# Three buffers for the modulation's weight tiles, and twelve K chunks of layer 0's output projection in three passes, in a two-layer hybrid decoder trunk

## Chip, cores and metric

The kernel runs on one core of a Trainium2 chip, as one program. The metric is the device time of the whole program in microseconds. Beside it stands the profile of one execution, from which all waits and busy times are read.

## What is computed

Two layers over 256 tokens of width 2048, all in float32. Each layer has a token mixer and a SwiGLU FFN, both behind an RMSNorm that is modulated by a conditioning vector. The mixer has three groups side by side (gated linear attention, sliding-window attention, gated DeltaNet), and one output projection.

```python
def reference(x, c, positions, w_mod, b_mod, ...):
    c_act = jax.nn.silu(c)
    for l in range(DEPTH):
        mod = c_act @ w_mod[l] + b_mod[l]
        shift1, scale1, gate1, shift2, scale2, gate2 = jnp.split(mod[:, None, :], 6, axis=-1)
        h = rms_norm(x, norm1_gain[l]) * (1.0 + scale1) + shift1
        x = x + gate1 * hybrid_token_mixer(h, positions, w_in[l], ..., w_out[l])
        h = rms_norm(x, norm2_gain[l]) * (1.0 + scale2) + shift2
        x = x + gate2 * swiglu_ffn(h, ffn_w_gate[l], ffn_w_up[l], ffn_w_down[l])
    return rms_norm(x, final_norm_gain)
```

In the mixer, `proj = h @ w_in` is cut into the groups' inputs, the group outputs are joined to 2048 columns (GLA the first 512, attention the next 1024, DeltaNet the last 512), and `mix @ w_out` follows. The GLA's decay comes from 16 columns of the projection times a 16 x 256 matrix, `gla_w_gk`.

## The kernel before

*Projections.* `stream` (a `gemm` is a stream of one group) walks over the 16 K chunks of 128 rows of a weight matrix. For each it loads 128 rows by 1024 columns (512 KB) into a `raw` tile, and multiplies for both 128-token blocks and both 512-column segments, that is four products, summed over K in PSUM tiles `acc` (L358). There are two ways to do a chunk:

- three passes: ScalarE rounds the tile to fp32r (`wh`, L330), VectorE takes the rest (`wl`, L331), and TensorE adds three products of high and low parts, 12 instructions a chunk;
- whole: the raw tile is used as it is in fp32, one product each, which the chip runs as two instructions. Then the tiles of `wh` and `wl` serve as landing places of raw weights too, in turn with `raw` (three each).

`WHOLE_OUT` says which 512-row groups of the output projection are whole: before, all four of layer 0 (0 GLA, 1 and 2 attention, 3 DeltaNet) and none of layer 1. The projection is done in two streams of two column halves each: K chunks 4 to 15, while the GLA is still running, then 0 to 3. For a group in three passes the activations are split too (`split_mix`, L392 and L393).

*Modulation.* `mod_segment` takes 16 steps for 1024 columns. Each loads a tile of `w_mod` of 512 KB (`mraw`, L220, pool `modp`) and adds it, times a value of c per partition, to `acc` on VectorE (L223, 128x1024). At the end, TensorE sums over partitions (L248, or L238 for gates, whose split also takes an `mraw` tile). The segments wait in a list (`mods`), and `tick` takes one out at a rate per weight chunk, so the modulation of later sub-layers is spread over the projections. Layer 0's first gate and second shift and scale (96 steps) must be done by its second norm.

*What sets the order.* All DMAs stand in one queue, SP's, and are issued strictly in its order: a load whose buffer is not free holds back all that stand behind it. The tile framework's scheduler decides in which order the instructions of each engine stand (the code's order is not it), so a pool's number of buffers moves instructions on every engine. The work that meets in the stretch of this change is the DeltaNet (its last VectorE row is L735), the sliding-window heads (L898 to L920), the last input projection (raw tiles 128x528), the GLA (L761 its product with `wgk`, then L764 to L842, levels L795, L798, L799, L804, L823, L831, and L515 at the end of each block), the output projection with its gated sum (L929, L931), and the second norm (L422, L441 to L451).

*Memory.* `kp` holds tiles for good: constants, `ones`, a rounded copy `ones_r`, the per-layer `small`, and `wgk` (the GLA's 16 x 256 matrix), loaded by `load_small` at the start of a layer.

Of the kernel before, what the change touches and what calls it, by code (L numbers as in the profile page):

```python
# [10 lines left out]
F32 = mybir.dt.float32  # L11
# [4 lines left out]
AF = mybir.ActivationFunctionType  # L16
# [3 lines left out]
P = 128  # L20
D = 2048
T = 256
# [20 lines left out]
WHOLE_IN = (True, False)  # L43
WHOLE_A = (3, 0)
RATE_LAST = 1.6
WHOLE_OUT = ((0, 1, 2, 3), ())
XN_ACT = ((False, False), (False, False))

FIN_LAG = 4
# [54 lines left out]
def trunk(ctx: ExitStack, tc, x, cT, pos, small, consts, b_mod, w_mod, w_in, w_gk, w_out,  # L104
# [2 lines left out]

    kp = ctx.enter_context(tc.tile_pool(name="kp", bufs=1))
    rawp = ctx.enter_context(tc.tile_pool(name="rawp", bufs=3))
    modp = ctx.enter_context(tc.tile_pool(name="modp", bufs=2))  # L110
    wsp = ctx.enter_context(tc.tile_pool(name="wsp", bufs=3))
    accp = ctx.enter_context(tc.tile_pool(name="accp", bufs=2))
    gatep = ctx.enter_context(tc.tile_pool(name="gatep", bufs=2))
# [13 lines left out]
    def tl(pool, shape, tag, dt=F32, bufs=None):  # L127
        return pool.tile(shape, dt, tag=tag, name=nm(tag), bufs=bufs)
# [11 lines left out]
    V, A, G, TE, SY = nc.vector, nc.scalar, nc.gpsimd, nc.tensor, nc.sync  # L140
# [19 lines left out]
        return ct[:, o:o + w] if o < N_FULL else masks[:, o - N_FULL:o - N_FULL + w]  # L160

    ident = cst("ident")
    ones = tl(kp, [P, P], "ones")
    G.memset(ones, 1.0)
    ones_r = tl(kp, [P, P], "ones_r", F32R)
    A.activation(ones_r, ones, AF.Copy)
    eps_t = tl(kp, [P, 1], "eps")
    G.memset(eps_t, EPS)
    half = tl(kp, [P, 16], "half")
# [287 lines left out]

    scr = [None, None]

    small_t, wgk_t = {}, {}  # L460
    gains = tl(kp, [P, DEPTH, 2 * KD], "gains")
    SY.dma_start(gains, small[:, :, :2 * KD].rearrange("l p n -> p l n"))

    def load_small(l):
        small_t[l] = tl(kp, [P, SMALL_W], "small")
        SY.dma_start(small_t[l], small[l][:, 2 * KD:])
        wgk_t[l] = tl(kp, [16, 256], "wgk")
        SY.dma_start(wgk_t[l], w_gk[l])

    def sm(l, name):  # L470
        o, w = SMALL[name]
# [17 lines left out]
    def to_mix(l, key, ps, gain=None):  # L489
        if key[1] == 0 and 0 not in WHOLE_OUT[l]:  # L490
            mix[key] = split(ps, gain)
# [37 lines left out]
    def gdn(l, pool, pc, zg, cbca):  # L529
# [3 lines left out]
        for gi, name in enumerate("qkv"):  # L533
            for c2 in range(2):
                ps = bank()
# [49 lines left out]
        ps = bank()  # L585
        for ni, name in enumerate("qk"):
            for c2 in range(2):
                sq = tl(pool, [P, 2, T], "g")
                A.activation(sq, hat[name, c2], AF.Square)
                for c in range(2):  # L590
                    for blk in range(NB):
                        n = ni * 8 + blk * 4 + c2 * 2 + c
                        TE.matmul(ps[:, n:n + 1], sq[:, c, blk * P:(blk + 1) * P],
                                  ones[:, 0:1], start=True, stop=True)
        ss = tl(smp, [P, 16], "qkss")
        V.tensor_scalar(ss, ps[:, :16], EPS, None, ALU.add)
        norms = tl(smp, [P, 8], "knorm")
# [12 lines left out]
        for blk in range(NB):  # L610
            ps = bank()
# [12 lines left out]
        for blk in range(NB):  # L624
# [4 lines left out]
            ps = bank()  # L629
# [7 lines left out]
            if blk == 0:  # L637
                ps = bank()
# [6 lines left out]
            else:  # L645
                ps = bank()
# [5 lines left out]
            ps = bank()  # L652
            for h in range(4):
                TE.matmul(ps[:, h * P:(h + 1) * P], ch("k", h, blk), ch("k", h, blk),
                          start=True, stop=True)
# [3 lines left out]
            ps = bank()  # L659
            for h in range(4):  # L660
                TE.matmul(ps[:, h * P:(h + 1) * P], ch("k", h, blk), ch("q", h, blk),
                          start=True, stop=True)
# [10 lines left out]
        for m in LEVELS[1:]:  # L673
            for blk in range(NB):
                ps = bank()
# [5 lines left out]
                ps = bank()  # L681
# [13 lines left out]
        for blk in range(NB):  # L695
            rhs = v_tok[blk]
            if blk == 1:
                ps = bank()
# [7 lines left out]
            ps = bank()  # L706
# [5 lines left out]
            if blk == 0:  # L712
                ps = bank()
# [5 lines left out]
                ps = bank()  # L719
# [4 lines left out]
            else:  # L724
                ps = bank()
# [5 lines left out]
                ps = bank()  # L731
# [6 lines left out]

    def gla(l, pool, qk_tok, v_tok, zg, lr):

        chan = []
        for i in range(2):
            ps = bank("ga")
# [10 lines left out]
        ps = bank("ga")  # L754
        for blk in range(NB):
            TE.transpose(ps[:16, blk * P:(blk + 1) * P], lr[blk], ident)
        lrT = tl(pool, [16, T], "lrT", bufs=1)
        A.activation(lrT, ps[:16, :T], AF.Copy)
        ps = bank("ga")
        for blk in range(NB):  # L760
            TE.matmul(ps[:, blk * T:(blk + 1) * T], lrT[:, blk * P:(blk + 1) * P], wgk_t[l],  # L761
                      start=True, stop=True)
        z = tl(pool, [P, NB, T], "a")
        V.tensor_tensor(z, ps.rearrange("p (b c) -> p b c", b=NB), bc(sm(l, "b_gk"), NB, 1),  # L764
# [7 lines left out]
        ps = bank("ga")  # L772
# [62 lines left out]
        for blk in range(NB):  # L835
            ps = bank("ga")
            for h in range(4):
                o = ps[:, h * P:(h + 1) * P]
                if blk == 1:
                    TE.matmul(o, cross[:, h % 2, h // 2], v_tok[0][:, h * P:(h + 1) * P],  # L840
                              start=True, stop=False)
                TE.matmul(o, Am[h % 2][:, h // 2, blk], v_tok[blk][:, h * P:(h + 1) * P],  # L842
                          start=blk == 0, stop=True)
# [374 lines left out]
```

## Time and profile before

| | us |
|---|---|
| median of 3 runs | 2584.6 |
| lowest, highest | 2583.5, 2589.6 |
| the profiled execution | 2585.3 |
| its span in the profile | 2583.5 |

Busy shares of the span: TensorE 94%, its weight loads 73%, VectorE 66%, ScalarE 41%, GpSimd 2%. HBM moved 233 GB/s on average, 600.8 MB in all.

How to read it: names like `acc<-wh,hm` are output and inputs in the program's names, L numbers are lines of the kernel before. In the wait views a line says who waited, for whom, how long in total, how often and the longest. In the stretch view a line gives the stretch, its length, then the busy time of TensorE (PE), its weight loads (PEld), VectorE (DVE), ScalarE (ACT) and GpSimd (POOL) with instruction counts, the granted TensorE clock as a share, the DMA engines' busy share and GB/s. SPq is SP's queue of DMAs.

### The profile page before, as it was taken

Reading aid. Unit: us, or ns where it says so; the run is one execution under the profiler, and the core shown is the slowest. Engines: PE = TensorE matmul, PEld = TensorE weight load, DVE = VectorE, ACT = ScalarE, POOL = GpSimd, SP = SyncE. Lnnn points to the kernel's source line nnn. Section 1 sums busy time; section 2 is a strip of 40 time slices with the busy share of each in tenths; the row PEclk is TensorE's granted clock in tenths of the full one; section 3 lists DMA queues with packets and bytes.
Section 4 is the critical chain, followed back from the end, with each engine's and each line's share of the span. In section 5 each row is a group of like instructions: output and inputs, shape, how many; then the busy total and the mean of one; then the engine's idle time right before and its main releaser. Section 6 shows DMA issues by size and latency. Waiting matters only on the chain.

```text
span 2583.5 us, 30803 instructions
## 1 busy us (share of the span) xinstructions
PE 2432.7 (94%) x11164; PEld 1884.1 (73%) x11164; DVE 1714.4 (66%) x2171; ACT 1053.5 (41%) x1548; POOL 58.2 (2%) x117
## 2 busy tenths in 40 slices
PE   4999998889999988999999999999999999999998
PEld 2555785447878767788877878877778878888876
DVE  6767867576675777657578785888664575544555
ACT  2203443124444333344335454564644434344443
POOL 1000000000000000000000000000000000000000
PEclk9999999989999999999999999999999999999999
DMA  9996538777778888868687861675676686666654
GB/s 341 368 322 204 180 114 282 258 231 268 261 259 260 283 268 274 292 193 286 223 277 261 281 192 50 214 232 192 212 256 193 200 286 195 188 191 188 189 184 155
DMA packets 190033, 600.79 MB, mean 233 GB/s; under 512 B 21628, under 2 KB 26268, under 8 KB 189496
## 3 DMA queue, kind: packets, MB, share of 16 engines
q1 hardware_dynamic: 189880, 598.81, 70.7%
q8 instruction: 88, 1.44, 0.2%
q14 instruction: 65, 0.53, 0.1%
HBM read 596.63 MB, written 2.10 MB: 232 GB/s over the span
## 4 chain that ended last, share of the span: by engine, by line
PE 57%; DMA 20%; DVE 10%; issue 8%; ACT 4%; POOL 1%; SPq 1%; DVEq 0%; ACTq 0%; POOLq 0%
PE acc L358 48%; DMA mraw<-in_w_mod 13%; DVE wl L331 4%; DMA raw<-in_w_down 3%; DMA raw<-in_w_in 2%; DVE acc L223 2%; ACT wh L330 1%; PE mm L403 1%; PE ga L895 1%; DMA raw<-in_w_up 1%; PE mm L678 1%; PE mm L685 1%; PE ga L916 1%; DMA raw<-in_w_gate 1%; PE fin L248 1%
## 5 line engine op out<-in xcount | busy, mean ns | idle before, releaser
L358 PE MATMUL acc<-wh,hm 128*128 128x512 f32 (+3 forms) x4872 | 1339.2, 389 | 20.9 <-DVE xs L931 4.7
L330 ACT ACTIVATE wh<-raw 128x1024 fp32r<-128x1024 f32 (+3 forms) x669 | 684.7, 1025 | 985.8 <-PE acc L358 548.9
L331 DVE TENSOR_TENSOR wl<-raw,wh 128x1024 fp32r<-128x1024 f32 (+3 forms) x669 | 785.2, 1179 | 446.6 <-ACT wh L330 444.5
L358 PEld LDWEIGHTS acc<-wh,hm 128*128 128x128 f32 x4872 | 892.0, 189 | 215.8 <-issue 25.5
L358 PE MATMUL acc<-wl,hm 128*128 128x512 f32 (+3 forms) x2484 | 792.3, 394 | 12.2 <-DVE wl L331 9.7
L223 DVE SCALAR_TENSOR_TENSOR acc<-mraw,c_act,acc 128x1024 f32<-128x1024 f32 x320 | 410.3, 1282 | 225.2 <-DMA mraw<-in_w_mod 222.9
L358 PEld LDWEIGHTS acc<-wl,hm 128*128 128x128 f32 x2484 | 458.4, 190 | 124.1 <-DVE wl L331 22.3
L358 PE MATMUL acc<-wh,ahl 128*128 128x512 f32 x560 | 158.4, 397 | 0.0
L358 PEld LDWEIGHTS acc<-wh,ahl 128*128 128x128 f32 x560 | 105.8, 189 | 24.5
L358 PE MATMUL acc<-wl,ahl 128*128 128x512 f32 x280 | 90.8, 398 | 7.2 <-DVE wl L331 7.2
L223 DVE SCALAR_TENSOR_TENSOR g<-g,c_act,g 128x512 f32<-128x512 f32 x128 | 88.7, 747 | 12.6 <-DMA g<-in_w_mod 12.4
L358 PE MATMUL acc<-wh,b 128*128 128x512 f32 (+2 forms) x184 | 74.7, 545 | 2.2 <-ACT b L447 2.1
L358 PE MATMUL acc<-wl,b 128*128 128x512 f32 (+2 forms) x176 | 67.1, 518 | 2.6 <-DVE g L969 2.6
L358 PEld LDWEIGHTS acc<-wl,ahl 128*128 128x128 f32 x280 | 52.2, 189 | 23.1 <-DVE wl L331 11.3
L358 PE MATMUL acc<-raw,b 128*128 128x512 f32 (+2 forms) x176 | 67.6, 524 | 0.0
L358 PEld LDWEIGHTS acc<-wh,b 128*128 128x128 f32 x184 | 35.2, 197 | 30.8 <-issue 23.1
L358 PEld LDWEIGHTS acc<-wl,b 128*128 128x128 f32 x176 | 32.8, 192 | 29.2 <-issue 20.3
L416 ACT ACTIVATE acc<-xs 128x512 f32<-128x512 f32 x32 | 19.0, 595 | 85.7 <-DVE xs L931 85.7
L447 ACT ACTIVATE b<-mm,mod,mod 128x128 f32<-128x128 f32 x24 | 9.2, 461 | 109.7 <-DVE mod L256 92.1
L358 PEld LDWEIGHTS acc<-raw,b 128*128 128x128 f32 x176 | 33.5, 195 | 26.7 <-issue 21.7
L929 DVE TENSOR_TENSOR acc<-acc,gate 128x512 f32<-128x512 f32 x64 | 43.0, 695 | 10.3 <-PE acc L358 10.2
L358 PE MATMUL acc<-raw,hm 128*128 128x512 f32 x88 | 41.7, 598 | 1.4 <-ACT acc L416 1.4
(314 smaller groups left out, 1645.8 us busy)
## 6 DMA issues: line engine op xcount, KB each, us to landing
mraw<-in_w_mod SPq DMA_DIRECT2D x320, 512.0 KB
raw<-in_w_down SPq DMA_DIRECT2D x176, 512.0 KB
raw<-in_w_gate SPq DMA_DIRECT2D x160, 512.0 KB
raw<-in_w_up SPq DMA_DIRECT2D x160, 512.0 KB
raw<-in_w_in SPq DMA_DIRECT2D x72, 512.0 KB
g<-in_w_mod SPq DMA_DIRECT2D x128, 256.0 KB
raw<-in_w_out SPq DMA_DIRECT2D x43, 512.0 KB
raw<-in_w_in SPq DMA_DIRECT2D x32, 264.0 KB
```

The costliest lines, as they stand in the source:

```text
L223: V.scalar_tensor_tensor(acc, raw[:, a], c_act[:, i + a:i + a + 1], acc, ALU.mult, ALU.add)
L248: TE.transpose(ps[:, i * P:(i + 1) * P], acc[:, (j + i) * P:(j + i + 1) * P], ident)
L330: A.activation(wh[:, :width], raw[:, :width], AF.Copy)
L331: V.tensor_tensor(wl[:, :width], raw[:, :width], wh[:, :width].bitcast(F32), ALU.subtract)
L358: TE.matmul(ps[blk, j][:, :segs[j][2]], xa, parts[j][part], start=i == 0 and n == 0, stop=last and n == len(terms) - 1)
L403: TE.transpose(ps[:, j * P:(j + 1) * P], src[:, j * P:(j + 1) * P], ident)
L416: A.activation(scr[0]() if junk is None else junk, xs[:, blk, j * 512:(j + 1) * 512], AF.Square, accum_out=ssq[blk][:, j:j + 1])
L678: TE.matmul(ps[:, s], LT[blk][:, s], Tm[blk][:, s], start=True, stop=True)
L685: TE.matmul(ps[:, s], U[blk][:, s], m1[:, s], start=True, stop=True)
L895: TE.matmul(ps[:, j * nk:(j + 1) * nk], qT[rows, i + j], kT[rows, g, :nk], start=True, stop=True)
L916: TE.matmul(ps[:, j * 64:(j + 1) * 64], pT[:, j * nk + kb * P:j * nk + (kb + 1) * P], kv[kb][:, P + g * 64:P + (g + 1) * 64], start=kb == ...
L929: V.tensor_tensor(ps, ps, need(gate_row, (l, part, j)), ALU.mult)
```

## The change

`modp` gets a third buffer. `WHOLE_OUT` for layer 0 keeps only group 0 whole, so twelve of sixteen chunks go through three passes. `ones` goes (`ones_r` is set to 1.0 directly and read as fp32 where `ones` was), and `wgk` moves into the GLA's own pool, loaded at the start of `gla`.

```diff
-WHOLE_OUT = ((0, 1, 2, 3), ())
+WHOLE_OUT = ((0,), ())
...
-    modp = ctx.enter_context(tc.tile_pool(name="modp", bufs=2))
+    modp = ctx.enter_context(tc.tile_pool(name="modp", bufs=3))
...
-    ones = tl(kp, [P, P], "ones")
-    G.memset(ones, 1.0)
     ones_r = tl(kp, [P, P], "ones_r", F32R)
-    A.activation(ones_r, ones, AF.Copy)
+    G.memset(ones_r.bitcast(F32), 1.0)
...
     def load_small(l):
         small_t[l] = tl(kp, [P, SMALL_W], "small")
         SY.dma_start(small_t[l], small[l][:, 2 * KD:])
-        wgk_t[l] = tl(kp, [16, 256], "wgk")
-        SY.dma_start(wgk_t[l], w_gk[l])
...
-                                  ones[:, 0:1], start=True, stop=True)
+                                  ones_r[:, 0:1].bitcast(F32), start=True, stop=True)
...
     def gla(l, pool, qk_tok, v_tok, zg, lr):
 
+        wgk = tl(pool, [16, T], "wgk", bufs=1)
+        SY.dma_start(wgk, w_gk[l])
...
-            TE.matmul(ps[:, blk * T:(blk + 1) * T], lrT[:, blk * P:(blk + 1) * P], wgk_t[l],
+            TE.matmul(ps[:, blk * T:(blk + 1) * T], lrT[:, blk * P:(blk + 1) * P], wgk,
```

The scheduler orders all engines anew. Lines after the change are two to four less than before (L220 is L218, L331 is L329, L323 is L321, L804 is L802). Three places show it. The first is SP's queue in layer 0, where the last input projection's loads (`raw` 128x528) meet the modulation's (`mraw`). Before:

```order
L323 DMA raw_2860<-in_w_in 128x528
L323 DMA raw_2881<-in_w_in 128x528
L323 DMA raw_2899<-in_w_in 128x528
L220 DMA mraw_2814<-in_w_mod 128x1024
L220 DMA mraw_2839<-in_w_mod 128x1024
L220 DMA mraw_2878<-in_w_mod 128x1024
L220 DMA mraw_2917<-in_w_mod 128x1024
L220 DMA mraw_2956<-in_w_mod 128x1024
L323 DMA raw_2920<-in_w_in 128x528
```

After, at the same loads (2856, 2877 and 2895 are 2860, 2881 and 2899 of before):

```order
L321 DMA raw_2856<-in_w_in 128x528
L218 DMA mraw_3012<-in_w_mod 128x1024
L218 DMA mraw_3051<-in_w_mod 128x1024
L321 DMA raw_2877<-in_w_in 128x528
L218 DMA mraw_3090<-in_w_mod 128x1024
L738 DMA wgk_3171<-in_w_gk 16x256
L218 DMA mraw_3137<-in_w_mod 128x1024
L218 DMA mraw_3452<-in_w_mod 128x1024
L218 DMA mraw_3455<-in_w_mod 128x1024
L321 DMA raw_2895<-in_w_in 128x528
```

The modulation's loads stood behind these weight loads and now stand between and ahead of them; by the end of the input projection seven more are issued. The GLA's small load stands among them.

The second is VectorE's queue at one level of layer 0's GLA (L804 and L795 are the level's products and differences, L831 its masked copies). Before:

```order
L795 TENSOR_TENSOR a_3260<-a_3186 128x512
L250 TENSOR_REDUCE sums_889_3476<-fin_3477 128x4
L223 SCALAR_TENSOR_TENSOR acc_3433<-mraw_3508,c_act_102,acc_3433 128x1024
L831 COPY_PREDICATED a_3188<-masks_90,ga_3248 128x512
L831 COPY_PREDICATED a_3189<-masks_90,mm_3249 128x512
L804 TENSOR_TENSOR a_3264<-a_3163,a_3260 128x32x8
L804 TENSOR_TENSOR a_3264<-a_3156,a_3260 128x32x8
```

After:

```order
L793 TENSOR_TENSOR a_3263<-a_3208 128x512
L221 SCALAR_TENSOR_TENSOR acc_3479<-mraw_3662,c_act_100,acc_3479 128x1024
L329 TENSOR_TENSOR wl_3671<-raw_3668,wh_3670 128x1024
L829 COPY_PREDICATED a_3210<-masks_90,ga_3251 128x512
L829 COPY_PREDICATED a_3211<-masks_90,mm_3252 128x512
L802 TENSOR_TENSOR a_3267<-a_3185,a_3263 128x64x4
L802 TENSOR_TENSOR a_3267<-a_3178,a_3263 128x64x4
```

A split of the output weights (L329, before L331) now stands beside the modulation's multiply inside the level.

The third is SP's queue in layer 0's FFN, in the third pair of gate and up projections. Before, a run without modulation:

```order
L323 DMA raw_5553<-in_w_gate 128x1024
L323 DMA raw_5571<-in_w_gate 128x1024
L323 DMA raw_5589<-in_w_gate 128x1024
L323 DMA raw_5628<-in_w_gate 128x1024
L323 DMA raw_5646<-in_w_gate 128x1024
L323 DMA raw_5667<-in_w_gate 128x1024
```

After:

```order
L218 DMA mraw_6235<-in_w_mod 128x1024
L321 DMA raw_5785<-in_w_gate 128x1024
L321 DMA raw_5803<-in_w_gate 128x1024
L218 DMA mraw_6274<-in_w_mod 128x1024
L321 DMA raw_5824<-in_w_gate 128x1024
L321 DMA raw_5842<-in_w_gate 128x1024
L218 DMA mraw_6331<-in_w_mod 128x1024
```

Modulation loads now stand here, one in three; eleven more are issued by the first load of the down projection.

More of the change, by code (lines that the diff above doesn't have):

```diff
@@ L458, in trunk @@
     scr = [None, None]
-    small_t, wgk_t = {}, {}
+    small_t = {}
     gains = tl(kp, [P, DEPTH, 2 * KD], "gains")
```

## Prediction

> **What bounds the kernel now.** I read the page first (busy time, the chain), then stretches of busy time for each stage, then the waits in those stretches, and last the order of instructions before and after.
>
> ```profile
> span 2583.5 us, 30803 instructions
> ...
> PE 2432.7 (94%) x11164; PEld 1884.1 (73%) x11164; DVE 1714.4 (66%) x2171; ACT 1053.5 (41%) x1548; POOL 58.2 (2%) x117
> PE 57%; DMA 20%; DVE 10%; issue 8%; ACT 4%; POOL 1%; SPq 1%; DVEq 0%; ACTq 0%; POOLq 0%
> PE acc L358 48%; DMA mraw<-in_w_mod 13%; DVE wl L331 4%; DMA raw<-in_w_down 3%; DMA raw<-in_w_in 2%; DVE acc L223 2%; ACT wh L330 1%; PE mm L403 1%; PE ga L895 1%; DMA raw<-in_w_up 1%; PE mm L678 1%; PE mm L685 1%; PE ga L916 1%; DMA raw<-in_w_gate 1%; PE fin L248 1%
> ```
>
> TensorE is busy for 94% of the span, so the whole kernel has 151 us of TensorE idle time to give (2583.5 less 2432.7). What stands out in the chain is 13% in loads of modulation weights: the stages in which those loads run are the ones to look at. The next view gives busy time by stretch (length, then PE, PEld, DVE, ACT, POOL, granted clock, DMA share, GB/s): first layer 0's mixer from the end of the delta rule to the second norm, then the same stretches of layer 1 (first edge the VectorE row L735, then L764, the second L515 of the GLA, the first L422 of the norm), then the others.
>
> ```profile
> 363.70:413.50 49.80, 45.73 (x311) 38.82 (x310) 36.07 (x55) 26.31 (x61) 2.76 (x4) 1.00 0.78 249
> 413.50:474.10 60.60, 55.00 (x257) 29.41 (x257) 45.82 (x71) 18.90 (x40) 3.98 (x3) 1.00 0.86 293
> 474.10:560.90 86.80, 75.80 (x186) 33.53 (x184) 57.97 (x70) 7.96 (x17) 1.90 (x2) 0.96 0.80 261
> 1618.70:1701.00 82.30, 79.26 (x482) 65.98 (x480) 63.41 (x90) 45.98 (x101) 6.91 (x9) 0.98 0.69 219
> 1701.00:1766.40 65.40, 59.97 (x353) 47.03 (x354) 59.15 (x85) 36.79 (x58) 2.94 (x2) 1.00 0.62 203
> 1766.40:1810.30 43.90, 40.42 (x175) 31.63 (x174) 35.46 (x50) 22.14 (x35) 0.96 (x1) 1.00 0.65 216
> ...
> 160.00:290.00 130.00, 122.96 (x456) 75.62 (x455) 94.71 (x212) 41.64 (x87) 5.19 (x6) 0.93 0.66 219
> 600.00:1110.00 510.00, 484.54 (x2103) 388.49 (x2101) 347.95 (x316) 201.06 (x208) 3.81 (x4) 0.99 0.82 273
> 1110.00:1290.00 180.00, 179.59 (x815) 147.78 (x814) 112.59 (x106) 75.82 (x79) 1.91 (x2) 1.00 0.73 235
> 1400.00:1500.00 100.00, 94.08 (x544) 80.45 (x543) 75.47 (x118) 47.45 (x69) 0.00 (x0) 1.00 0.89 286
> 1676.00:1830.00 154.00, 139.59 (x753) 111.71 (x752) 125.15 (x181) 90.96 (x163) 5.96 (x6) 0.97 0.60 198
> 2060.00:2130.00 70.00, 67.29 (x305) 55.24 (x304) 49.62 (x46) 27.89 (x29) 0.00 (x0) 1.00 0.84 287
> ```
>
> In layer 0's output projection (474 to 561) TensorE works 75.8 of 86.8 us on one-instruction-pair fp32 products, and VectorE is free for a third of the time. Within it, the chain alternates for 35 us between a modulation load and the multiply that frees its buffer:
>
> ```profile
> 481.93 5.50 DMA mraw<-in_w_mod
> ...
> 511.26 4.29 DMA mraw<-in_w_mod
> 515.55 0.03 issue
> 515.60 0.04 issue
> 515.65 1.30 DVE acc L223
> ```
>
> From 481.93 to 511.26 there are five such turns, 5.87 us each, and each moves two modulation tiles and about one of the output weights: two buffers set that pace. In layer 0's FFN (600 to 1110) 25.5 us of TensorE are idle, against 0.4 us in 1110 to 1290. Who waits there:
>
> ```profile
> PEld acc L358 <- DVE wl L331: 22.3, 26, 2.4
> SPq L323 <- DVE wl L331: 320.2, 165, 4.2
> SPq L220 <- DVE acc L223: 31.7, 28, 2.1
> ACT wh L330 <- DMA raw<-in_w_down: 68.9, 30, 5.7
> DVE acc L223 <- DMA mraw<-in_w_mod: 93.8, 68, 3.6
> ```
>
> VectorE stands 93.8 us in a multiply whose tile has not landed; the split for the next weights (L331) is queued behind it, and TensorE waits for the split.
>
> **The change, part by part.** Durations:
>
> ```profile
> 488.72 3.60 PE L358 MATMUL acc<-wl,hm 128*128 128x512 f32 x8
> 492.15 3.60 PE L358 MATMUL acc<-raw,hm 128*128 128x512 f32 x8
> 2236.02 86.31 PE acc L358 x379
> 475.30 0.66 PE ga L403 x4
> L331 DVE TENSOR_TENSOR wl<-raw,wh 128x1024 fp32r<-128x1024 f32 x605 | 736.7, 1223 | 435.6 <-ACT wh L330 434.3
> L223 DVE SCALAR_TENSOR_TENSOR acc<-mraw,c_act,acc 128x1024 f32<-128x1024 f32 x320 | 410.3, 1282 | 225.2 <-DMA mraw<-in_w_mod 222.9 <-DMA acc<-in_b_mod 0.2
> L393 DVE TENSOR_TENSOR hm<-hm,hm x6: 682/684/686, 1673.4 to 1687.4; 128x512 fp32r<-128x512 f32 x6
> ```
>
> *Split on TensorE.* One chunk by one half in whole fp32 is four products, eight instructions, and starts 3.43 us after the one before it (492.15 less 488.72). In three passes it is twelve at 0.228 us (86.31/379), 2.73 us. Twelve chunks by two halves: 24 x 0.70 = 17 us less TensorE work. The Trainium skill ("FP8 and Floating Point Precision", TensorE Precision Notes) says that true FP32 makes four passes through the array; at 0.228 us each that would be 3.65 us a step and 22 us saved. The rows say 3.43, so 17 stands.
>
> *Split on VectorE and ScalarE.* 24 x 1.223 + 6 x 0.684 = 33.5 us more VectorE work, and about as many ScalarE instructions; ScalarE is busy 8 of 87 us there and takes them. VectorE is strict in its order, so I added up the rows of both orders between the same edges: VectorE's each at its mean duration from the groups (means include overlap, so sums run up to a tenth over busy time), TensorE's at 0.228 us for 512 columns in one pass, 0.858 (3.43/4) in whole fp32 and 0.165 (0.66/4) for a 128-column fp32 product. VectorE before: 39.1, 51.0, 61.6 us in the three stretches; after: 50.9, 66.2, 63.9. TensorE before 42.3, 48.8, 77.3; after 50.4, 46.4, 59.9. The largest of the two per stretch comes to 170.6 before and 181.0 after: TensorE's 17 us are outdone by VectorE.
>
> How much longer than that sum the stretches last is the open size. Before it is 197.2/170.6 = 1.16; at the same ratios, stretch by stretch, after would take 59.9 + 78.7 + 71.8 = 210. Layer 1 already splits its whole output projection; its VectorE sums are 68.4, 66.3 and 38.5 for 82.3, 65.4 and 43.9 us. At those ratios after takes 61.2 + 65.3 + 72.9 = 199. With no slack at all it would be 181. I take layer 1's, since it is the same code with the same splits: 199 against 197, +2. Bounds -16 and +13.
>
> *Modulation moved ahead.* Seven modulation steps now stand before L735 and two A-projection splits after it.
>
> ```profile
> 320.00:360.00 40.00, 39.82 (x285) 34.25 (x283) 21.25 (x40) 18.04 (x51) 2.41 (x4) 1.00 0.11 28
> ```
>
> From 320 to 360 DMA runs at 28 GB/s and VectorE is half free, while TensorE is dense: cover for 7 x 1.28 us. TensorE's rows ahead of L734 shrink by 6.6 us (moved behind it). So L735 comes between 6.6 us earlier (TensorE sets it) and 9 us later (every added multiply sits in the delta rule's serial chain); I take 5 earlier, as TensorE is at 99.6%. With the +2 the mixer gives -3, between -23 and +22. From the first L422 on, the second norm's rows are the same: nothing.
>
> *Layer 0's FFN.* Of 25.5 us idle, at most the waits for L331 (22.3 at the weight loads, which overlap other work) can go; the rest are fill and evacuation. With a third buffer a modulation tile is issued one step earlier in SP's order, and the 93.8 us of waiting multiplies, 1.4 us each over 68, mostly land within one more turn. Bounds 0 and -20; I take -8, a third of the idle time, since SP's own waits are ten to one for weight tiles (320.2 against 31.7) and the third buffer does not touch those. Eleven modulation steps also leave the down projection's stretch for the gate and up stretch.
>
> *160 to 290* (last input block, same two-buffer turns): 7.0 us idle, between 0 and -7, I take -2. *Layer 1* (1400 to 1500, 1676 to 1830, 2060 to 2130): 5.9 + 14.4 + 2.7 = 23 us idle, but weights rather than modulation are late in most of it and its VectorE sums hardly change (173.2 before, 173.8 after); between +3 and -10, I take -3.
>
> *The rest.* The dropped copy of the ones (one 128x128 ScalarE instruction) stood under the load of x at the start:
>
> ```profile
> 2.12 8.08 DMA xs<-in_x
> ```
>
> so it is worth nothing. The GLA's small weight load (16 KB, two in all) moves to SP's queue among the A projection's loads. In layer 0 it waits for a ScalarE square of the delta rule's last gate; behind it stand ten weight loads that TensorE needs. At that place SP already waits for buffers and TensorE does not notice (39.82 of 40 above), and the load's user stands just ahead of the edge at 413.5, a whole stretch later: nothing, at worst one SP turn of 5 us. In layer 1 it waits for nothing.
>
> Sum: -2 - 3 - 8 - 3 = -16 against the profiled execution's 2585.3 us (span 2583.5, 1.8 us around it; 0.7 above the median of 2584.6): 2569.
>
> **Rivals.** *VectorE becomes the bound in the GLA (slower).* The GLA is a serial chain VectorE, ScalarE, TensorE, VectorE, level by level; in front of each level there now stand a multiply and a split, 2.5 us, where there was a multiply alone. Before, VectorE is already full in the middle of it:
>
> ```profile
> 440.00:460.00 20.00, 17.92 (x98) 9.39 (x96) 19.44 (x33) 5.75 (x10) 0.95 (x1) 1.00 0.91 316
> ```
>
> If the ratios of before hold (210) and the earlier multiplies delay the delta rule by 9 us, the mixer loses 13 + 9 = 22, and with -13 from elsewhere the kernel takes 2594. It decides from the point where L735 to L422 takes over some 216 us. Against it: layer 1's GLA, as loaded (66.3), takes 65.4. The Trainium skill ("TensorE: Matmul & The Clock Gate", in the section on the array's sub-arrays) calls ScalarE and VectorE strict FIFOs; the multiplies that wait 93.8 us with splits behind them agree, and it is what makes this rival possible.
>
> *The third buffer changes nothing.* SP is held by weight tiles, and a modulation load that stands behind one goes no earlier, whatever its buffer. Then early, FFN and layer 1 terms are zero and only the mixer's -3 stays: 2582. For it: 320.2 against 31.7 us of SP waits. Against it: the turns of 5.87 us, where SP waits for the multiply.
>
> *All slack goes.* The last stretch stops turning on two buffers and lasts its 64 us of VectorE rows, the mixer gives -20, the FFN -14, the early part -4, layer 1 -5: 2542. For it: all three resources (60 us TensorE, 64 VectorE) are even there. Against it: no stretch of either layer's mixer but layer 1's GLA comes within a tenth of its sum.
>
> **How the numbers follow.** My forecast 0.55, VectorE-bound 0.13, no effect of the buffer 0.20, all slack 0.12. About 0.3% (7.75 us) can be told from no change. Faster: 0.9 of the forecast's chance, all of the last, a fifth of the third: 0.65. Slower: the first rival and a little: 0.14. Same: 0.21. The forecast's own range is 2558 to 2580; for 8 in 10 it must reach most of both outer cases: 2546 to 2592.
>
> **What would show it.** Right: in layer 0, L735 to L422 about 199 us, L735 at about 359; the DMA share from 320 to 360 well above 0.11; 24 more 128x1024 rows of L331; fewer whole fp32 products; VectorE's waits for modulation tiles in the FFN at half of 93.8 us or less, TensorE idle there near 17 us. Wrong: the GLA over 72 us long (first rival); FFN waits unchanged (second); the mixer's last stretch under 66 us (third). A changed time in 1110 to 1290, where nothing is moved, would mean a cause that I have not seen.

## The result, and the profile after

The changed kernel takes 2563.9 us (median of 4 runs, 2560.5 to 2566.4), the kernel before 2584.1 beside it (2578.1 to 2589.6): ratio 0.9916, 95% interval 0.9892 to 0.9940, 20 us faster. The forecast was 2569, range 2546 to 2592. Total and sign held; of the terms that made them up, most were mis-sized, and one lay outside its bounds. One run of the kernel with only the room, below, took 7672 us and is left out of its median. The profiled execution after took 2560.5 us, 24.8 less than the one profiled before, so the stages below add up to 24.8 and not to 20.

Head and two groups of the page after (weight splits, modulation's multiplies):

```profile
span 2558.7 us, 31074 instructions
...
PE 2412.8 (94%) x11260; PEld 1903.4 (74%) x11260; DVE 1745.6 (68%) x2201; ACT 1079.6 (42%) x1576; POOL 58.3 (2%) x117
...
L329 DVE TENSOR_TENSOR wl<-raw,wh 128x1024 fp32r<-128x1024 f32 (+3 forms) x693 | 815.4, 1181 | 472.9 <-ACT wh L328 471.0
L221 DVE SCALAR_TENSOR_TENSOR acc<-mraw,c_act,acc 128x1024 f32<-128x1024 f32 x320 | 409.9, 1281 | 133.2 <-DMA mraw<-in_w_mod 130.8
```

VectorE's idle time in front of the modulation's multiplies fell from 225.2 to 133.2 us, and VectorE has 31 us more work (1714.4 before). Busy time by stretch after, with edges at the same instructions as before: the last input block up to the first mask of the delta rule (L680 before, L676 now), the stretch inside the delta rule, the mixer's three stretches (L731 to L762, to the GLA's second L513, to L420), layer 0's FFN, and the stretch in which nothing is moved.

```profile
160.00:276.60 116.60, 113.61 (x430) 67.11 (x429) 90.00 (x207) 39.61 (x84) 4.73 (x6) 0.99 0.69 231
320.00:360.00 40.00, 37.93 (x258) 32.56 (x257) 27.03 (x51) 20.85 (x59) 2.90 (x6) 1.00 0.47 135
349.50:406.40 56.90, 54.47 (x360) 46.74 (x360) 47.11 (x71) 36.08 (x83) 2.20 (x5) 1.00 0.81 256
406.40:475.20 68.80, 56.12 (x319) 44.34 (x319) 58.94 (x88) 32.40 (x53) 4.92 (x4) 0.88 0.64 206
475.20:554.40 79.20, 63.61 (x199) 38.58 (x198) 59.91 (x68) 14.47 (x24) 1.79 (x2) 0.91 0.77 269
593.00:1085.00 492.00, 478.76 (x2109) 390.11 (x2108) 349.41 (x317) 200.93 (x209) 3.83 (x4) 0.99 0.83 283
1085.00:1265.00 180.00, 178.96 (x812) 147.55 (x811) 113.00 (x106) 75.38 (x79) 1.91 (x2) 1.00 0.73 235
```

The waits after in 593 to 1085, which answer to those shown of before in the FFN:

```profile
PEld acc L356 <- DVE wl L329: 6.4, 8, 1.6
SPq L321 <- DVE wl L329: 328.2, 171, 5.7
SPq L218 <- DVE acc L221: 29.3, 25, 1.9
DVE acc L221 <- DMA mraw<-in_w_mod: 66.0, 51, 3.3
```

Stage by stage, in us of the two profiled executions:

| stage | before | after | shift | forecast |
|---|---|---|---|---|
| start to the first L680 | 289.7 | 276.6 | -13.1 | -2 |
| L680 to L735 (delta rule) | 74.0 | 72.9 | -1.1 | -5 |
| L735 to L422 (GLA, output projection) | 197.2 | 204.9 | +7.7 | +2 |
| L422 to the end of layer 0 (FFN) | 805.6 | 787.7 | -17.9 | -8 |
| layer 1 and the end | 1217.0 | 1216.6 | -0.4 | -3 |

### The profile page after: what moved, and what is told of

It is laid out like the page before. It is cut to its first block, busy times and chain, and to the rows that moved or that the text cites. A ratio compares the mean times of both kernels' runs of the same rounds, so it can differ in the third digit from the quotient of the medians.

```text
span 2558.7 us, 31074 instructions
## 1 busy us (share of the span) xinstructions
PE 2412.8 (94%) x11260; PEld 1903.4 (74%) x11260; DVE 1745.6 (68%) x2201; ACT 1079.6 (42%) x1576; POOL 58.3 (2%) x117
## 3 DMA queue, kind: packets, MB, share of 16 engines
q1 hardware_dynamic: 189880, 598.81, 71.1%
## 5 line engine op out<-in xcount | busy, mean ns | idle before, releaser
L356 PE MATMUL acc<-wh,hm 128*128 128x512 f32 (+3 forms) x5000 | 1363.3, 386 | 28.5 <-ACT wh L328 13.8
L329 DVE TENSOR_TENSOR wl<-raw,wh 128x1024 fp32r<-128x1024 f32 (+3 forms) x693 | 815.4, 1181 | 472.9 <-ACT wh L328 471.0
L328 ACT ACTIVATE wh<-raw 128x1024 fp32r<-128x1024 f32 (+3 forms) x693 | 710.4, 1027 | 1007.2 <-PE acc L356 616.8
L356 PEld LDWEIGHTS acc<-wh,hm 128*128 128x128 f32 x5000 | 916.1, 189 | 220.3 <-ACT wh L328 19.0
L356 PE MATMUL acc<-wl,hm 128*128 128x512 f32 (+2 forms) x2516 | 794.8, 389 | 9.4 <-DVE wl L329 7.9
L356 PEld LDWEIGHTS acc<-wl,hm 128*128 128x128 f32 x2516 | 464.8, 189 | 111.5 <-DVE wl L329 17.2
L221 DVE SCALAR_TENSOR_TENSOR acc<-mraw,c_act,acc 128x1024 f32<-128x1024 f32 x320 | 409.9, 1281 | 133.2 <-DMA mraw<-in_w_mod 130.8
L356 PE MATMUL acc<-raw,b 128*128 128x512 f32 (+2 forms) x176 | 66.7, 517 | 0.0
L356 PEld LDWEIGHTS acc<-wl,ahl 128*128 128x128 f32 x280 | 52.5, 189 | 16.3 <-DVE wl L329 4.1
L929 DVE TENSOR_TENSOR xs<-xs,acc 128x512 f32<-128x512 f32 x64 | 41.5, 678 | 0.0
L210 POOL MEMSET acc<- 128x1024 f32 x20 | 19.0, 955 | 961.3 <-PE fin L246 651.2
```

The lines of the kernel that those rows point to most:

```text
L210: G.memset(st["acc"][:, :width], 0.0)
L221: V.scalar_tensor_tensor(acc, raw[:, a], c_act[:, i + a:i + a + 1], acc, ALU.mult, ALU.add)
L328: A.activation(wh[:, :width], raw[:, :width], AF.Copy)
L329: V.tensor_tensor(wl[:, :width], raw[:, :width], wh[:, :width].bitcast(F32), ALU.subtract)
L356: TE.matmul(ps[blk, j][:, :segs[j][2]], xa, parts[j][part], start=i == 0 and n == 0, stop=last and n == len(terms) - 1)
L929: V.tensor_tensor(x_j, x_j, ps, ALU.add)
```

## The experiments

Five questions: which part of the change gains, why the other part costs, whether VectorE's work or the weights' landing places are behind that cost, what the third buffer does in the FFN, and what the one queue of loads costs. All kernels stand beside runs of the kernel before (2581 to 2584 us in each set). Intervals are of the ratio to it.

| kernel | median | ratio, 95% interval |
|---|---|---|
| room only (two buffers, no split) | 2578.8 | 0.9987, 0.9969 to 1.0005 |
| third buffer alone | 2548.6 | 0.9864, 0.9840 to 0.9888 |
| split alone | 2586.8 | 1.0016, 1.0000 to 1.0031 |
| the change (both) | 2563.9 | 0.9916, 0.9892 to 0.9940 |
| split, fourth raw buffer for the third modulation buffer | 2581.2 | 0.9997, 0.9980 to 1.0013 |
| third buffer, landing in raw only | 2549.7 | 0.9865, 0.9838 to 0.9892 |
| the same, with splits that nobody reads | 2563.7 | 0.9925, 0.9900 to 0.9951 |
| third buffer, second half split | 2561.9 | 0.9913, 0.9889 to 0.9936 |
| two buffers, modulation steps moved | 2577.9 | 0.9980, 0.9962 to 0.9998 |
| the change, earlier modulation | 2551.6 | 0.9885, 0.9861 to 0.9908 |
| third buffer alone, earlier modulation | 2555.8 | 0.9898, 0.9874 to 0.9922 |
| third buffer, four chunks split | 2545.7 | 0.9861, 0.9837 to 0.9886 |
| the change, modulation in GpSimd's queue | 2649.2 | 1.0262, 1.0233 to 1.0292 |

How far one profiled execution can be trusted: layer 1 does the same work in all of these but the last, and its part of the span reads 1217 to 1229 us. Some profiled executions lie well off their kernel's median (the split alone 2596.3 against 2586.8, the third buffer alone 2555.2 against 2548.6). A single stage is taken as different below only where several kernels agree or where medians say it.

### The parts alone

Room only:

```diff
-WHOLE_OUT = ((0,), ())
+WHOLE_OUT = ((0, 1, 2, 3), ())
...
-    modp = ctx.enter_context(tc.tile_pool(name="modp", bufs=3))
+    modp = ctx.enter_context(tc.tile_pool(name="modp", bufs=2))
```

> Only the room made for the buffer: the ones tile dropped and the small GLA matrix loaded inside the GLA, two modulation buffers, whole fp32 in all of layer 0's output projection, as before. Theory A (third buffer) and theory B (split) both expect the time of before, 2584 us within 5, and L735 at about 364 us. Theory C (the moved small load and the new order of instructions are what gains): 2572 or less, with L735 near 350.

Third buffer alone, against the changed kernel:

```diff
-WHOLE_OUT = ((0,), ())
+WHOLE_OUT = ((0, 1, 2, 3), ())
```

> Third modulation buffer, no split: all of layer 0's output projection stays whole fp32. Theory A (the third buffer gives the gain, in the early input blocks and in layer 0's first down projection, the split gives next to nothing): 2560 to 2569 us, L735 14 us earlier than before, the first down projection some 17 us shorter, L735 to L422 about 197 us or less as VectorE has fewer splits. Theory B (the 17 us of TensorE work saved by the split are the gain): 2580 us or more, L735 earlier but the time given back at the whole-fp32 output projection.

Split alone:

```diff
-    modp = ctx.enter_context(tc.tile_pool(name="modp", bufs=3))
+    modp = ctx.enter_context(tc.tile_pool(name="modp", bufs=2))
```

> The split alone, two modulation buffers. Theory A: 2580 to 2592 us, L735 at about 364, L735 to L422 197 to 210 us with VectorE the busiest engine, waits of multiplies for modulation tiles in layer 0's FFN at 90 us or more as before. Theory B: 2563 to 2570 us, L735 to L422 about 180 us.

The room cannot be told from no change (2578.8). From there the third buffer gives 30 us by the medians (2548.6; 32 by the ratios). By the medians the split costs 8 us with two buffers (2586.8, intervals just overlapping) and 15 with three (2563.9 against 2548.6; the runs, 2560 to 2566 and 2542 to 2555, do not overlap). So the change is a gain of 30 and a loss of 15. Theory A held for the buffer, though its 2560 to 2569 us was too slow, and it missed the loss. Theories B and C fell. The rows of the mixer (L735 to L422) and of the FFN, first room only, then the third buffer alone:

```profile
360.00:559.80 199.80, 179.74 (x751) 102.88 (x749) 139.72 (x194) 53.09 (x118) 8.64 (x9) 0.97 0.80 264
559.80:1361.10 801.30, 768.08 (x3343) 619.57 (x3344) 542.75 (x519) 329.99 (x378) 9.07 (x11) 0.98 0.78 260
```

```profile
349.60:538.40 188.80, 179.33 (x783) 106.84 (x783) 138.18 (x197) 56.78 (x130) 8.04 (x11) 0.99 0.79 268
538.40:1327.50 789.10, 762.13 (x3344) 615.91 (x3343) 540.54 (x513) 330.58 (x379) 8.13 (x10) 0.99 0.79 265
```

The changed kernel's mixer in one row, and that of the split alone:

```profile
349.50:554.40 204.90, 174.19 (x875) 129.66 (x875) 165.95 (x225) 82.96 (x160) 8.91 (x10) 0.93 0.73 244
```

```profile
359.50:562.50 203.00, 168.09 (x847) 122.04 (x845) 166.67 (x221) 78.72 (x147) 6.49 (x9) 0.95 0.77 254
```

The third buffer brings the mixer from 199.8 to 188.8 without the split, and nothing with it (203.0, 204.9). TensorE's busy time times its granted clock is 179.33 x 0.99 = 177.5 with the buffer alone and 174.19 x 0.93 = 162.0 after: 15.5 us less work by this estimate, near the 17 of the forecast. But VectorE has 28 us more (165.95 less 138.18), and TensorE ran at 0.93, so that only 5 us of it show as busy time and none as length.

### A raw buffer for the same room

```diff
-    rawp = ctx.enter_context(tc.tile_pool(name="rawp", bufs=3))
-    modp = ctx.enter_context(tc.tile_pool(name="modp", bufs=3))
+    rawp = ctx.enter_context(tc.tile_pool(name="rawp", bufs=4))
+    modp = ctx.enter_context(tc.tile_pool(name="modp", bufs=2))
```

> The changed kernel with two modulation buffers, and its room (4 KB a partition) given to a fourth raw weight buffer instead. Theory A (SP's queue turns on the modulation buffers): at most half of the gain, 2572 us or more, and multiplies still wait 80 us or more for modulation tiles in layer 0's FFN. Rival D (any extra landing place gives the gain, since SP waits ten times longer for weight buffers than for modulation buffers): 2565 us or less.

Theory A held and rival D fell: 2581.2, 6 us under the split with three raw buffers and 17 over the change. Between 593 and 1085 multiplies still wait 91.1 us for modulation tiles. Yet it does something in one place: behind the GLA, where ScalarE rounds the output weights, it waits half as long for them. After the change, from 475.2 to 554.4:

```profile
ACT wh L328 <- DMA raw<-in_w_out: 32.8, 7, 6.5
```

With four raw buffers, from 478.3 to 546.7:

```profile
ACT wh L328 <- DMA raw<-in_w_out: 15.3, 7, 3.1
```

That stretch takes 68.4 us there, against 79.2 after the change and 85.4 with the split alone, and the mixer 185.2, but the FFN takes 806.9. This points to late weights as a second limit behind the GLA, beside VectorE.

### VectorE's rows or the landing places

Whole chunks land in nine tiles (raw, wh and wl), split chunks in three. Either this or VectorE's 33 us could be the split's cost. First the third buffer alone with three places for the twelve chunks:

```diff
-            if k in whole:
+            if k in whole and k not in only_raw:
                 which[1] += 1
...
+                   only_raw=range(4, 16) if l == 0 else (),
```

> The kernel with the third buffer alone (whole fp32 everywhere in layer 0's output projection), but the twelve chunks that the change splits may land only in the three raw tiles, as they must when they are split; before, and with the buffer alone, they have nine places. Theory V (the GLA grew from 56 to 69 us by the split's VectorE rows): the GLA stretch (L764 to the second L515) stays at 54 to 60 us, 2543 to 2556 us. Theory L (it grew because the split takes six of nine landing places from the weights): 65 us or more, 2558 to 2567 us.

2549.7: six places fewer cost 1 us. Theory L fell on the time. In the profiled execution the GLA stretch rose to 61.6 us from 55.9 (granted clock 0.94, not 1.00), 2 over what V allowed, and the mixer to 194.9 from 188.8; the medians do not show it. Then the same with the 24 splits made and not used:

```diff
+            if k in only_raw:
+                wh = tl(wsp, [P, 1024], "wh", F32R)
+                wl = tl(wsp, [P, 1024], "wl", F32R)
+                A.activation(wh, raw, AF.Copy)
+                V.tensor_tensor(wl, raw, wh.bitcast(F32), ALU.subtract)
             if k in whole:
                 return [(r, None) for r, _ in cuts]
```

> As the one before (third buffer, three landing places), and ScalarE and VectorE also split the 24 tiles of the twelve chunks; the products are whole fp32 all the same, so nobody reads the split halves: the split's cost without its 17 us less TensorE work (the six splits of the activations are left out). Theory V: the GLA 65 to 70 us, 10 to 14 us longer than in the kernel before this one, and 2560 to 2580 us. Theory L: no longer than the kernel before this one, within 5 us.

2563.7, 14 us more than without the splits (runs 2545 to 2555 and 2560 to 2572): theory V by the time. The GLA stretch (L764 to the second L515) of the kernel without and of the kernel with them:

```profile
405.00:466.60 61.60, 54.42 (x250) 29.83 (x248) 43.78 (x70) 18.81 (x40) 2.99 (x3) 0.94 0.78 264
```

```profile
405.40:472.10 66.70, 59.64 (x276) 31.40 (x275) 61.29 (x90) 32.02 (x53) 4.03 (x4) 1.00 0.64 210
```

VectorE goes from 71% to 92% busy. The stretch is 5 us longer, not the 10 to 14 that theory V had named (11 against the 55.9 of the kernel with nine places), so the place of the other microseconds is not shown. ScalarE's roundings came with the splits, but VectorE waits for ScalarE only 3.5 us in the 66.7, so they do not fill this stretch. And the change itself, which does the same splits and six more of activations (some 4 us), and saves TensorE its 17 us, takes 2563.9: the saving buys no more than those six.

### Modulation out of VectorE's way

If VectorE's crowding is the cause, the split should pay once modulation steps leave the GLA:

```diff
-RATE_LAST = 1.6
+RATE_LAST = 2.0
```

> The changed kernel with the rate of modulation steps in layer 0's last input block at 2.0 instead of 1.6 per weight chunk: eleven to twelve steps of modulation (about 15 us of VectorE multiplies) stand before L735 and L764 instead of inside the GLA and the output projection. Theory V (in the mixer the split's VectorE rows and the modulation's crowd each other): L735 to L422 188 to 197 us instead of 205, L735 at most 5 us later, 2550 to 2560 us. Rival T (the mixer is set by TensorE's order and late output weights, not by VectorE): L735 to L422 200 us or more, 2561 to 2570 us.

> The same rate of 2.0 with the third buffer alone (no split). Without the split VectorE is 138 of 189 us busy from L735 to L422, so theory V expects little: L735 to L422 183 to 190 us, 2542 to 2551 us. Rival T: within 3 us of 2549 us too; a loss of over 5 us would mean that the delta rule, ahead of L735, has no room for eleven more multiplies.

L735 to L422 in the changed kernel with the higher rate, and in the one without the split:

```profile
358.60:545.20 186.60, 167.74 (x873) 125.08 (x873) 154.17 (x215) 84.18 (x159) 10.74 (x11) 0.95 0.72 236
```

```profile
358.90:542.80 183.90, 174.55 (x776) 103.03 (x777) 124.14 (x186) 54.78 (x127) 9.90 (x11) 1.00 0.70 239
```

With the split the mixer loses 18 us and the kernel 12 (2551.6), as theory V had it, but not in the GLA. The GLA and the stretch behind it, with the split and the higher rate:

```profile
417.70:489.00 71.30, 65.61 (x368) 51.71 (x366) 63.67 (x89) 34.58 (x56) 3.84 (x2) 0.93 0.67 216
489.00:545.20 56.20, 45.91 (x133) 25.02 (x134) 39.90 (x50) 11.17 (x20) 1.91 (x2) 0.91 0.71 244
```

The GLA still holds 16 multiplies of the modulation, has 15 splits instead of 10, and takes 71.3 us instead of 68.8. Behind it stand 13 multiplies and 6 splits instead of 25 and 11, and that stretch takes 56.2 us instead of 79.2, with 20 us less VectorE work (39.90, 59.91 after the change). So the modulation left the output projection behind the GLA, not the GLA.

Without the split the mixer loses 5, and the kernel takes 7 us more (2555.8, over the 2542 to 2551 expected), since L735 comes 9 us later in both: five extra multiplies in the last input block cost 4 us and six in the delta rule 5, where 5 was expected at most for all.

In the mixer the split costs 3 us with modulation early (186.6 against 183.9), and 16 with modulation as it was (204.9 against 188.8). That the kernel with the split is 4 us faster with modulation early does not show that the split wins there: the runs overlap, and in the profiled executions the difference comes from the FFN (782 against 790 us), where both do the same work.

### Fewer splits

Four chunks, those of the DeltaNet, which are last in each half:

```diff
-WHOLE_OUT = ((0,), ())
+WHOLE_OUT = ((0, 1, 2), ())
```

> Third buffer, and only the DeltaNet's four chunks (12 to 15) go through three passes: 8 splits of weights and 2 of activations, not 24 and 6. If the split's cost goes with its VectorE rows (15 us for 33.5 us of rows): 2552 to 2556 us. If it comes with the first splits that fall into the GLA or behind it, since the raw tiles then land in three places (as with twelve splits in the second half, 2562): 2557 to 2565 us. If a few splits are worth it for TensorE (5.6 us less work): 2543 to 2547 us.

2545.7, the fastest median of all, though not to be told from the third buffer alone. The first two cases fell: eight splits do not cost a third of the loss, nor more. The mixer's row:

```profile
349.20:535.30 186.10, 174.39 (x819) 111.37 (x819) 147.29 (x207) 65.62 (x140) 7.81 (x11) 0.99 0.80 272
```

Twelve chunks of the second half only:

```diff
+                stream(groups[:1], ks, lhs_mix, whole=ks)
+                stream(groups[1:], ks, lhs_mix, whole=())
```

> Third buffer; of the twelve chunks only those of the second column half go through three passes, which mostly run after the GLA, and those of the first half stay whole fp32. Twelve splits of weights, not 24, and activations are split after the GLA's code. Theory V with room behind the GLA: GLA 55 to 60 us, L515 to L422 70 to 78 us instead of 80, 2540 to 2549 us. Rival (VectorE is as full behind the GLA as in it, so that a split costs there too): L515 to L422 83 us or more, 2552 to 2565 us.

This kernel also takes the two halves as two streams, and splits the activations after the GLA's code. 2561.9: the time of the rival, but not its place. Behind the GLA the stretch is 76.4 us, as theory V had it; 5 us are lost before the GLA and 9 in it, where VectorE is only 50.8 of 64.7 us busy. The 5 us ahead of the GLA are the same TensorE work at a lower granted clock (53.90 us busy at 0.94, where the third buffer alone has 50.74 at 1.00). In the GLA, VectorE waits 9.6 us for the GLA's product with `wgk`, 4.9 with the third buffer alone. Half the splits cost nearly all of the loss, so crowding by the count of VectorE rows does not cover this case, and its cause stays open.

### Where the steps stand, or how many buffers

In the FFN the third buffer also moved eleven modulation steps from the first down projection into gate and up. With two buffers and rates that do the same:

```diff
+                            if l == 0 and chunks[0] == 0 and rate[1] == RATE_FFN[0]:
+                                rate[1] = 0.54
...
+                if l == 0:
+                    rate[1] = RATE_FFN[0] if final else 0.17
```

> Two modulation buffers, no split, the room as after; the rates of modulation steps per weight chunk in layer 0's FFN are 0.54 for 0.4 in gate and up before the first down projection, and 0.17 in that projection, so that 217 steps are issued by its first load, as with three buffers, instead of 206. Theory M (the FFN's gain comes from where the steps stand, not from the buffer): L422 to the end of layer 0 787 to 792 us (801 with two buffers, 789 with three), kernel 2566 to 2574 us. Theory N (the buffer itself lets multiplies wait less): 798 to 806 us, what the first down projection gains lost again in gate and up; kernel 2577 to 2588 us.

L422 to the end of layer 0:

```profile
558.50:1359.80 801.30, 768.92 (x3338) 619.68 (x3339) 542.02 (x517) 329.94 (x379) 8.51 (x10) 0.98 0.78 260
```

Not a tenth of a microsecond less than with the steps where they were: the down projection became 8 us shorter (67.8 against 75.6 between its halves' ends) and the rest lost it again. Theory N. All kernels with two modulation buffers read 801 to 807 us here, all with three in SP's queue 782 to 792, whatever their output projection: the gain comes from the buffer, not from the place of the steps.

### A queue of its own for the modulation

After the change, in the GLA, slices of ten microseconds:

```profile
425.00:435.00 10.00, 9.37 (x68) 7.33 (x67) 10.00 (x17) 4.79 (x7) 0.00 (x0) 1.00 0.67 213
435.00:445.00 10.00, 9.23 (x64) 6.94 (x63) 10.00 (x15) 4.80 (x7) 0.00 (x0) 1.00 0.69 213
445.00:455.00 10.00, 7.04 (x56) 5.43 (x54) 9.52 (x17) 5.49 (x8) 0.00 (x0) 0.85 0.55 181
455.00:465.00 10.00, 5.02 (x20) 3.78 (x20) 7.15 (x15) 2.13 (x10) 1.98 (x1) 0.64 0.05 5
465.00:475.00 10.00, 8.57 (x37) 7.46 (x38) 7.21 (x10) 3.22 (x10) 1.78 (x1) 0.66 0.76 243
```

SP's queue in its timeline there (start, length, issues), and VectorE's:

```profile
446.95 0.33 SPq L321 DMA_DIRECT2D raw<-in_w_out  x1
450.63 16.51 SPq L218 DMA_DIRECT2D mraw<-in_w_mod  x3
468.00 0.33 SPq L321 DMA_DIRECT2D raw<-in_w_out  x1
```

```profile
449.28 1.32 DVE L221 SCALAR_TENSOR_TENSOR acc<-mraw,c_act,acc 128x1024 f32<-128x1024 f32 x1
...
458.99 1.27 DVE L929 TENSOR_TENSOR xs<-xs,acc 128x512 f32<-128x512 f32 x2
462.20 0.17 DVE L504 TENSOR_SCALAR gss<-gss 128x4 f32<-128x4 f32 x1 [1.94 <-ACT a L499]
462.28 1.28 DVE L221 SCALAR_TENSOR_TENSOR acc<-mraw,c_act,acc 128x1024 f32<-128x1024 f32 x1
464.47 1.12 DVE L511 SCALAR_TENSOR_TENSOR a<-ga,grs,hm 128x128 f32<-128x128 f32 x4 [0.92 <-POOL grs L406]
465.51 1.27 DVE L221 SCALAR_TENSOR_TENSOR acc<-mraw,c_act,acc 128x1024 f32<-128x1024 f32 x1
```

VectorE is full to 455, then works off the GLA's serial end, and reads no modulation tile from 450.6 to 462.3. SP stands before the next modulation loads for 16.5 us (12.5 in its longest wait); the output weights are behind them in its order, and from 447 to 468 none is issued. DMA falls to 5 GB/s and TensorE to half. With the third buffer alone SP's longest such wait from 430 to 470 is 4.3 us. So in this execution modulation loads stood ahead of weights in SP's order, and VectorE was late to free their buffers. This gap is not the split's cost as such: the idle splits cost 14 us with a longest wait for a modulation buffer of 4.4 us there (430 to 485), and the change with earlier modulation has one of 16.3 us and is 12 us faster. The test moves the loads of the three-buffer pool out of SP's queue:

```diff
-            SY.dma_start(raw, w_mod[l, i * P:(i + n) * P, c0:c0 + width]
+            (SY if early else G).dma_start(raw, w_mod[l, i * P:(i + n) * P, c0:c0 + width]
```

> The changed kernel with the modulation's tile loads (those of the three-buffer pool) in GpSimd's DMA queue instead of SP's, so that a load that waits for a multiply no longer holds back weight loads that stand behind it; GpSimd's own small operations now stand behind such loads. Theory Q (after the change SP stands 16.5 us, from 450.6 to 467, in front of modulation loads whose buffers VectorE has not read, and the output weights behind them come late: DMA share 0.05, TensorE half idle): DMA share over 0.3 throughout the GLA, L735 to L422 185 to 197 us instead of 205, and less waiting for weights in layer 0's FFN; 2535 to 2556 us. Rival (weights and modulation share the same DMA engines, so a load that goes earlier only takes from another): 2558 to 2570 us. Third (GpSimd's operations of the attention and of the GLA's norm come late behind waiting loads): over 2572 us, with long waits for them ahead of L735 or at the GLA's end.

L735 to L422, then the queue's waits over the whole span:

```profile
380.80:556.80 176.00, 152.43 (x781) 112.76 (x781) 150.77 (x207) 74.11 (x136) 33.40 (x55) 0.94 0.73 249
```

```profile
POOL mraw L218 <- DVE acc L221: 894.9, 255, 58.5
```

The mixer is 29 us shorter than after the change, the shortest of all, as theory Q had it (the DMA share over the GLA is 0.61, and 0.43 from 470 to 480, in the part of the GLA that answers to the gap). The 29 us are not the queue's alone: L735 comes 31 us later, and eight of the 55 multiplies of the modulation have moved ahead of it, so that L422 comes 2 us later than after the change. The kernel is 85 us slower, as the third theory had it, though only in part at its places: 23 us up to the delta rule and 9 in it, but also 46 in layer 0's FFN (833.8 us) and 41 in layer 1. That ScalarE waits longer for gate and up weights in layer 0's FFN (104.5 us for up against 71.1) is seen; why they come late is open.

## Why the prediction came out right, and where its terms failed

*Mechanism of the change.* The split's TensorE saving was forecast at 17 us and is 15.5 in work. The 24 more splits (669 to 693) and VectorE's extra 33.5 us (31 over the span) came as worked out. "TensorE's 17 us are outdone by VectorE" held in its sign: the idle split costs 14 us, and TensorE's saving on top of it buys no more than the six splits of activations. The half split, with a loss of 13 us, is not covered by it.

*L735 to L422, +2.* It came to 204.9, not 199. The step that failed is the choice of layer 1's ratios of length to VectorE work. By stretch they gave 61.2, 65.3 and 72.9 us, and 56.9, 68.8 and 79.2 came: the miss is in the GLA and, most of it, behind it. Layer 1 was no likeness there: in the profile before, its GLA holds 11 multiplies of the modulation and the stretch behind it 4, where layer 0 after the change has 16 and 25. With 13 multiplies and 6 splits behind the GLA that stretch took 56.2 us, and with a fourth raw buffer 68.4; how the miss divides between VectorE's rows and late weights is open. The first rival was therefore partly true: the GLA went from 60.6 to 68.8 us, under the 72 it named, and the mixer stayed under the 216 from which it decides. That a third buffer would give 11 us here without the split was not seen at all, since the two parts were summed in one row count.

*Early part, -2 with 0 to -7.* It was -13, outside its bounds, and 9.4 of that against the kernel with the room only. The bound was TensorE's idle time, 7.0 us, and that was the error: its busy time can shrink too. Before, two slices read:

```profile
250.00:270.00 20.00, 20.00 (x99) 15.52 (x98) 13.78 (x41) 9.16 (x23) 3.56 (x3) 0.83 0.38 112
270.00:290.00 20.00, 15.60 (x86) 12.76 (x86) 16.37 (x28) 6.91 (x17) 0.46 (x1) 0.83 0.56 174
```

After, from 160 to the same instruction the clock is 0.99 and TensorE 113.6 us busy, where it was 0.93 and 123.0 up to 290. The waits for modulation tiles in that part, 16.2 us in all (12 times), became 7.0 (4 times).

*L735, 5 earlier through TensorE's shorter rows.* The delta rule lost 1.1 us; L735 came 14.2 us earlier, nearly all brought from ahead of it. The added multiplies were hidden, as said: the delta rule holds 16 instead of 7. The DMA share from 320 to 360 rose from 0.11 to 0.47, as asked for, though that window now reaches 10 us past L735; over the whole delta rule it rose from 0.35 to 0.54. Eleven more, in the kernels with the higher rate, were not hidden.

*FFN, -8 of at most -20.* It was -17.9 in these executions, 12 and 16 against kernels that differ by the buffer alone. "A third of the idle time" was too little. The rows from L422 to the end of layer 0, before and after:

```profile
560.90:1366.50 805.60, 767.58 (x3342) 616.27 (x3343) 543.07 (x519) 329.53 (x378) 9.06 (x11) 0.98 0.78 259
```

```profile
554.40:1342.10 787.70, 763.32 (x3348) 617.87 (x3348) 543.70 (x516) 331.59 (x380) 9.09 (x11) 0.99 0.79 266
```

TensorE's idle time (length less busy time) fell from 38.0 to 24.4 us and its busy time by 4.3, its waits for splits from 22.3 to 6.4 in the narrower stretch. Yet VectorE's waits for modulation tiles fell only from 93.8 to 66.0, not to half, and SP's waits hardly moved (320.2 and 328.2 for weights, 31.7 and 29.3 for modulation). So the forecast's signs of it were wrong in size though the gain was larger. VectorE waits less often (51 times, not 68). That fewer of its waits reach TensorE through a split behind them, and that this is the path by which the buffer gains, is argued from these rows, not tested apart.

*No effect of the buffer (the second rival)* is refuted by 30 us. *All slack goes* is refuted in the mixer (last stretch 79.2, not under 66). *Layer 1, -3*: none seen, and 1085 to 1265 unchanged (178.96 of 180), as asked for.

So 2569 came out near 2564 in good part by luck, because errors of both signs met: the buffer's gain was taken as 18 us (2 early, 5 at L735, 8 in the FFN, 3 in layer 1) and is 30, the split was taken as a loss of 2 and costs 15.

## What to carry to other kernels

Two parts of one change are costed apart and together: here a buffer worth 30 us was joined to a split that cost 15, and leaving out all or most of the split (2549, 2546) beats the change. Work moved from TensorE to VectorE is worth what VectorE has free in that stretch, and the other work queued there counts: the same split cost the mixer 16 us, or 3 with part of the modulation moved ahead. In one in-order queue of loads, look for the stretch in which a load waits for a busy engine and ask what stands behind it, but cost the cure over the whole kernel: a queue of its own shortened the mixer by 29 us and cost 85 in all.

## What the runs showed of the hardware

The granted clock carries part of what a shorter wait is worth. In the early part (160 to the first L680) TensorE's busy time fell by 9 us, from 122.7 to 113.6, at nearly the same work (busy time times clock: 114 and 112 us). In kernels that take all twelve chunks in three passes the clock was 0.93 to 0.95 over the mixer, 0.97 to 1.00 in those that take none of them so: 0.05 of 174 us is 9 us of TensorE work. Before the change, fine slices show it at half twice between 240 and 288:

```profile
252.00:256.00 4.00, 4.00 (x13) 3.04 (x14) 0.76 (x5) 0.63 (x1) 3.08 (x2) 0.50 0.00 0
...
272.00:276.00 4.00, 1.04 (x4) 0.64 (x4) 4.00 (x7) 0.39 (x1) 0.00 (x0) 0.83 0.46 132
276.00:280.00 4.00, 3.36 (x7) 2.11 (x8) 3.39 (x8) 1.75 (x9) 0.00 (x0) 0.50 0.64 151
280.00:284.00 4.00, 4.00 (x29) 3.75 (x28) 2.95 (x8) 1.26 (x3) 0.00 (x0) 0.82 0.63 245
284.00:288.00 4.00, 4.00 (x23) 3.36 (x23) 4.00 (x7) 1.07 (x1) 0.46 (x1) 1.00 0.45 133
```

The second fall comes after TensorE stood idle, 3.3 us from 271.2: 1.04 us of work in 4, then half clock, and full clock eight microseconds on. The Trainium skill ("TensorE: Matmul & The Clock Gate", Part 1) says that an idle window of about 3.4 us halves the array's clock and a busy one frees it; this fall agrees. So here an idle stretch of a few microseconds cost TensorE more than its length, and idle time in the profile is not the most that a shorter wait can give. The first fall has no idle time in the profile: TensorE's row from 248.17 on is 32 products of one column each, 4.46 us long, and why the clock fell there no run shows. No run here changed the clock by itself, so how much of the third buffer's 30 us came that way is not separated.

That modulation loads in GpSimd's queue, with 229 us of that engine busy where it was 58, would slow stages as far away as layer 1 (by 41 us) was not expected either.
